# Gated product of two column halves, one core: the first row's load as two transfers of 32 and 96 partitions

## The chip, the cores and the metric

The kernel runs on one core of a Trainium2 chip. The metric is device time in microseconds (us) of one execution; three executions of the kernel before gave 932.57, 932.62 and 932.98, with a median of 932.62 us. One execution was recorded by the hardware profiler; its numbers are called the profile, and answers drawn from the recording are called the trace.

## The reference

```
x = randn(8192, 8192), float32
a, b = split(x, 2, axis=-1)          # columns 0..4095 and 4096..8191
out = a * (1 / (1 + exp(-b)))        # 8192 x 4096, float32
```

Every element of x is read once (268 MB) and every element of the output is written once (134 MB). There is no reuse: the sigmoid and the product take one element of each half.

## The kernel before, in words

**Tiles.** A tile is 256 rows of x: 128 partitions with two rows (`r`) each, so 64 KB of input and 32 KB of output per partition, 8 MB in and 4 MB out per tile. There are 32 tiles. Two input slots `xs[0]`, `xs[1]` and two output slots `os[0]`, `os[1]` are used in turn (`SLOTS = 2`). Neighbouring partitions of a tile lie 128 KB apart in x.

**One tile's work.** `load(i)` (L59 to L64) issues the input transfer on SP's queue. `work(i, ...)` (L72 to L93) has ACT put the sigmoid over the second column half in place (L82), and then DVE and POOL multiply the two halves into the output slot (L91); POOL takes 3/16 of the columns from tile 2 to tile 30, DVE the rest. `store(i, ...)` (L66 to L70) issues the output transfer on ACT's queue.

**Pieces.** Lists say how each tile is cut. `loads[0]` is `rows`: the first tile's input goes as two transfers, row 0 of every partition (32 KB each on 128 partitions, 4 MB) and then row 1. All other tiles load in one transfer of 8 MB. The first and the last tile are worked on in four pieces (`fourths`), and stored in two and three transfers.

**Order.** The loop issues `load(0)` and `load(1)`, and then for each tile its work, `load(i + 2)`, and its stores. `place` (L48 to L57) keeps the program order and drops all dependencies but the ones that it is given: a load waits for the multiplications that last read its slot (`free`, L62), the sigmoid waits for the transfers that bring its piece (`landed`, L78) and for the store that frees the output slot (`gone`, L79), a multiplication waits for the sigmoid, and a store for the multiplications.

**The early launch.** `_launch_early` (L110 to L120) takes the first transfer that SP issues, and it alone, out of the body and puts it ahead of the barrier at which the engines meet on entry, so that it is issued at the very start of the span. All other loads follow behind the barrier. `_close_on_sync` shortens the end and is not touched by the change.

**Transfers in the profile.** Each transfer of 128 partitions shows in the count of DMA packets as 144 packets: one data packet for each partition and 16 small ones of completion (33 loads make the 4752 packets of the input queue, 35 stores the 5040 of the output queue).

Of the kernel before, what the change touches and what calls it, by code (L numbers as in the profile page):

```python
# [8 lines left out]
def _tiles(ctx, tc, x, out):  # L9
    nc = tc.nc  # L10
    P = nc.NUM_PARTITIONS
    DEP = mybir.DependencyInfo(mybir.DependencyClass.Sync, mybir.DependencyReason.DATA)
    fp32 = mybir.dt.float32
    SIG = mybir.ActivationFunctionType.Sigmoid

    n_rows, n_cols = x.shape
    half = n_cols // 2
    R = 2
    SLOTS = 2
    n_tiles = n_rows // (P * R)  # L20
    x_g = x.rearrange("(g p h r) m -> g h p (r m)", p=P, h=2, r=R)
    out_g = out.rearrange("(g p h r) m -> g h p (r m)", p=P, h=2, r=R)

    pool = ctx.enter_context(tc.tile_pool(name="io", bufs=1))
    xs = [pool.tile([P, R * n_cols], fp32, name=f"x_sb{k}") for k in range(SLOTS)]
    os = [pool.tile([P, R * half], fp32, name=f"o_sb{k}") for k in range(SLOTS)]

    whole = [(0, 8)]
    rows = [(0, 4), (4, 8)]
    cut = half // 16 * 3  # L30
    at_once = [(0, 8, 0, half)]
    fourths = [(k, k + 2, k % 4 * half // 4, (k % 4 + 2) * half // 4) for k in range(0, 8, 2)]
    loads = [whole] * n_tiles
    works = [at_once] * n_tiles
    stores = [whole] * n_tiles
    behind = [0] * n_tiles
    loads[0] = stores[0] = rows
    works[0] = works[-1] = fourths
    stores[-1] = [(0, 4), (4, 6), (6, 8)]
    behind[-1] = 1  # L40

    def meet(a, b):
        return a[0] < b[1] and b[0] < a[1]

    traced = [[] for _ in range(SLOTS)]
    load_of, mul_of, store_of = {}, {}, {}

    def place(i, ins, *needs):  # L48


        kept = {n.ins.name for n in needs}
        for e in traced[i % SLOTS]:
            if e.ins.name not in kept:
                tc.declare_no_dep(ins.ins, e.ins, reason="follows from the waits that are kept")
        traced[i % SLOTS].append(ins)
        tc.keep_in_program_order(ins)
        return ins  # L57

    def load(i):  # L59
        for lo, hi in loads[i]:  # L60
            c = slice(lo * n_cols // 4, hi * n_cols // 4)
            free = [m for w, m in mul_of.get(i - SLOTS, []) if meet(w, (lo, hi))]  # L62
            ins = nc.sync.dma_start(out=xs[i % SLOTS][:, c], in_=x_g[i // 2, i % 2, :, c])  # L63
            load_of.setdefault(i, []).append(((lo, hi), place(i, ins, *free)))  # L64

    def store(i, lo, hi):  # L66
        c = slice(lo * half // 4, hi * half // 4)
        ins = nc.scalar.dma_start(out=out_g[i // 2, i % 2, :, c], in_=os[i % SLOTS][:, c])  # L68
        done = [m for w, m in mul_of[i] if meet(w, (lo, hi))]
        store_of.setdefault(i, []).append(((lo, hi), place(i, ins, *done)))  # L70

    def work(i, lo, hi, near, far):  # L72

        rows = xs[i % SLOTS].rearrange("p (r h m) -> p r h m", r=R, h=2)
        packed = os[i % SLOTS].rearrange("p (r m) -> p r m", r=R)
        r, c = slice(lo // 4, (hi + 3) // 4), slice(near, far)
        b = rows[:, r, 1, c]
        landed = [s for w, s in load_of[i] if meet(w, (lo, hi))]  # L78
        gone = [s for w, s in store_of.get(i - SLOTS, []) if meet(w, (lo, hi))]  # L79
        by_sigmoid = 0 < i < n_tiles - 1  # L80
        needs = [*landed, *(gone if by_sigmoid else ())]
        sig = place(i, nc.scalar.activation(out=b, in_=b, func=SIG), *needs)  # L82
        shares = [(nc.vector, near, far)]
        if by_sigmoid and i > 1:
            shares = [(nc.gpsimd, near, cut), (nc.vector, cut, far)]
        if by_sigmoid:
            for s in gone:
                tc.add_manual_dep(sig.ins, s.ins.name, DEP, reason="frees the output slot")
        for engine, a, z in shares:
            part = slice(a, z)  # L90
            mul = engine.tensor_mul(out=packed[:, r, part], in0=rows[:, r, 0, part], in1=rows[:, r, 1, part])  # L91
            place(i, mul, sig, *(() if by_sigmoid else gone))
            mul_of.setdefault(i, []).append(((lo, hi), mul))  # L93

    for i in range(SLOTS):
        load(i)
    for i in range(n_tiles):
        due = list(stores[i])
        for k, piece in enumerate(works[i]):
            work(i, *piece)  # L100
            ready = works[i][k - behind[i]][1] if k >= behind[i] else 0
            while len(stores[i]) > 1 and k < len(works[i]) - 1 and due[0][1] <= ready:
                store(i, *due.pop(0))
        if i + SLOTS < n_tiles:
            load(i + SLOTS)
        for lo, hi in due:
            store(i, lo, hi)
# [115 lines left out]
```

## Time and profile before

| what | value |
|---|---|
| median of three executions | 932.62 us |
| the profiled execution's own time | 932.69 us |
| its span, first to last instruction | 931.3 us |
| DVE, ACT, POOL busy | 232.3, 227.0, 299.5 us (25%, 24%, 32%) |
| moved by DMA | 402.67 MB, mean 432 GB/s over the span |
| first row of tile 0: ACT starts on it | 11.95 us |
| second row of tile 0: ACT starts on it | 21.67 us |
| tile 1: ACT starts on it | 46.39 us |
| last load issued, landed | 871.48, 911.8 us |

The profiled execution took 1.4 us more than its span, which is what lies around the first and the last instruction. In views by stretches, the DMA share is the time of the packets that start in the stretch, over 16 engines; short stretches can be over 1 or under it only because packets begin on one side of the border and end on the other. In the view of DMA issues, "us to landing" runs from the issue to the last completion.

### The profile page before, as it was taken

What the parts mean: (1) busy time and instruction counts of PE and PEld (TensorE: products, weight loads), DVE (VectorE), ACT (ScalarE), POOL (GpSimd) and SP (SyncE); (2) the same over time, 40 slices, a digit from 0 to 9 for tenths busy, and PEclk for the clock granted to TensorE, in tenths of its full rate; (3) what the DMA queues carried; (4) which work ended last, traced back from release to release, by engine and by line L of the source; (5) the groups of instructions that cost most, each with busy time, mean ns of one, the idle gap of its engine ahead of it and who ended that gap; (6) DMA issues with size and microseconds to landing.
All of it is one profiled execution on the core that took longest, in us unless ns stands there. A gap on an engine that the chain in (4) does not pass through costs nothing.

```text
span 931.3 us, 294 instructions
## 1 busy us (share of the span) xinstructions
DVE 232.3 (25%) x38; ACT 227.0 (24%) x39; POOL 299.5 (32%) x33
## 2 busy tenths in 40 slices
DVE  1133311333113331133321333203332033320233
ACT  2023332033320333202332023320233302333023
POOL 0004412444124441244422444224442244421440
DMA  9999999999999999999999999999999999999998
GB/s 405 450 405 450 428 450 408 470 405 428 450 428 450 405 462 417 428 450 426 452 405 436 442 428 450 418 457 408 428 450 426 452 407 466 411 428 450 425 453 383
DMA packets 9793, 402.67 MB, mean 432 GB/s; under 512 B 1088, under 2 KB 1088, under 8 KB 1088
## 3 DMA queue, kind: packets, MB, share of 16 engines
q1 hardware_dynamic: 4752, 268.44, 66.6%
q10 hardware_dynamic: 5040, 134.22, 33.4%
q14 instruction: 1, 0.01, 0.0%
HBM read 268.44 MB, written 134.22 MB: 432 GB/s over the span
## 4 chain that ended last, share of the span: by engine, by line
DMA 70%; POOL 16%; ACT 12%; DVE 2%; issue 0%; ACTq 0%; SPq 0%
DMA out_dram<-o_sb 61%; POOL o_sb L91 16%; ACT x_sb L82 12%; DMA x_sb<-in_x_dram 9%; DVE o_sb L91 2%; ACTq L68 0%; SPq L63 0%
## 5 line engine op out<-in xcount | busy, mean ns | idle before, releaser
L91 POOL TENSOR_TENSOR o_sb<-x_sb 128x1536 f32<-128x1536 f32 x29 | 299.3, 10321 | 600.7 <-ACT x_sb L82 600.7
L91 DVE TENSOR_TENSOR o_sb<-x_sb 128x6656 f32<-128x6656 f32 (+2 forms) x38 | 232.3, 6123 | 690.6 <-ACT x_sb L82 690.6
L82 ACT ACTIVATE x_sb<-x_sb 128x8192 f32<-128x8192 f32 (+1 forms) x38 | 225.7, 5950 | 692.9 <-DMA out_dram<-o_sb 632.8
L82 ACT ACT_TABLE_LOAD x1 | 1.3, 1283 | 0.8 <-PEq L207 0.8
L207 POOL MEMSET const-float32-0.0<- 128x1 f32 x1 | 0.1, 98 | 0.2 <-issue 0.2
L207 POOL MEMSET const-bfloat16-1.0<- 128x1 bf16 x1 | 0.1, 101 | 0.0
L207 POOL MEMSET const-uint8-127<- 128x1 uint8 x1 | 0.1, 101 | 0.0
L207 POOL MEMSET const-float32-1.0<- 128x1 f32 x1 | 0.1, 98 | 0.0
## 6 DMA issues: line engine op xcount, KB each, us to landing
out_dram<-o_sb ACTq DMA_DIRECT2D x30, 4096.0 KB, 40.5
x_sb<-in_x_dram SPq DMA_DIRECT2D x2, 4096.0 KB, 16.4
out_dram<-o_sb ACTq DMA_DIRECT2D x3, 2048.0 KB, 28.1
out_dram<-o_sb ACTq DMA_DIRECT2D x2, 1024.0 KB, 8.3
x_sb<-in_x_dram SPq DMA_DIRECT2D x31, 40.3
```

Of the source, the lines that this page charges most:

```text
L82: sig = place(i, nc.scalar.activation(out=b, in_=b, func=SIG), *needs)
L91: mul = engine.tensor_mul(out=packed[:, r, part], in0=rows[:, r, 0, part], in1=rows[:, r, 1, part])
L207: nc = _bacc.Bacc("TRN2", target_bir_lowering=False, num_devices=1)
```

## The change

The first transfer of the first tile, row 0 of its 128 partitions, is issued as two transfers: one of partitions 0 to 31 (1 MB) and one of partitions 32 to 127 (3 MB). All other transfers stay as they were. `_launch_early` still takes the first transfer that SP issues, which is now the one of 32 partitions; the one of 96 partitions is issued behind the barrier, ahead of row 1's. Both are entered in `load_of[0]`, so the sigmoids on row 0 wait for both.

```diff
         for lo, hi in loads[i]:
             c = slice(lo * n_cols // 4, hi * n_cols // 4)
             free = [m for w, m in mul_of.get(i - SLOTS, []) if meet(w, (lo, hi))]
-            ins = nc.sync.dma_start(out=xs[i % SLOTS][:, c], in_=x_g[i // 2, i % 2, :, c])
-            load_of.setdefault(i, []).append(((lo, hi), place(i, ins, *free)))
+            for p, q in [(0, 32), (32, P)] if i == 0 and lo == 0 else [(0, P)]:
+                ins = nc.sync.dma_start(out=xs[i % SLOTS][p:q, c], in_=x_g[i // 2, i % 2, p:q, c])
+                load_of.setdefault(i, []).append(((lo, hi), place(i, ins, *free)))
```

In the compiled order of instructions SP has one transfer more. The wait for the second transfer of row 0 is put on ACT's table load, the instruction ahead of the first sigmoid, which had no wait before; the sigmoid itself waits for the first. The transfers take the completion semaphores in turn, so from there on each transfer uses the next one in the circle.

## Prediction

> **What bounds the kernel now.** I read the page's row of DMA slices first, then the trace by stretches, then the first stretches' packets, and last the timeline of the start and the waits.
>
> The page's span, its DMA slices and its packet count:
>
> ```profile
> span 931.3 us, 294 instructions
> DMA  9999999999999999999999999999999999999998
> DMA packets 9793, 402.67 MB, mean 432 GB/s; under 512 B 1088, under 2 KB 1088, under 8 KB 1088
> ```
>
> No slice but the last has the 16 DMA engines under 90% busy, while no compute engine is busy for more than a third of the span. By stretches (columns: stretch, length, busy time and instructions of DVE, ACT and POOL, clock, DMA share, GB/s):
>
> ```profile
> 0.00:1.00 1.00, 0.00 (x0) 0.22 (x1) 0.20 (x4) 1.00 0.00 0
> 1.00:2.00 1.00, 0.00 (x0) 1.00 (x1) 0.00 (x0) 1.00 1.76 524
> ...
> 46.00:104.00 58.00, 15.78 (x2) 18.26 (x3) 10.32 (x1) 1.00 0.99 426
> 104.00:162.00 58.00, 14.19 (x2) 14.06 (x3) 20.64 (x2) 1.00 1.00 434
> 162.00:510.00 348.00, 85.11 (x12) 84.04 (x13) 123.86 (x12) 1.00 1.00 434
> 510.00:858.00 348.00, 85.11 (x12) 84.43 (x13) 123.86 (x12) 1.00 1.00 434
> ```
>
> The DMA engines move nothing in the first microsecond, and from then on their share is 1.00: 434 GB/s in every long stretch. There is no slack in them to take up a late start, so time that all of them lose anywhere is time on the end. The chain of waits names ACT and POOL between the stores, but the DMA engines work on other tiles' transfers meanwhile.
>
> How one engine works is read from the packets that start between 1 and 2 us and between 2 and 11.2 us:
>
> ```profile
> DMA packets 16, 0.52 MB, mean 524 GB/s; under 512 B 0, under 2 KB 0, under 8 KB 0
> q1 hardware_dynamic: 16, 0.52, 175.7%
> ```
>
> ```profile
> DMA packets 112, 3.67 MB, mean 399 GB/s; under 512 B 0, under 2 KB 0, under 8 KB 0
> q1 hardware_dynamic: 112, 3.67, 92.3%
> ```
>
> The first 16 packets, one per engine, took 1.76 us each (175.7% of 1 us). The other 112 packets of row 0 took 0.923 x 9.2 us x 16 / 112 = 1.21 us each. A packet is 32 KB, one partition's row, so an engine writes one partition at a time, at 27 GB/s, and sixteen do it side by side. The timeline of the start:
>
> ```profile
> 0.78 1.28 ACT L82 ACT_TABLE_LOAD   x1 [0.78 <-PEq L207]
> 11.95 3.71 ACT L82 ACTIVATE x_sb<-x_sb 128x2048 f32<-128x2048 f32 x2 [9.89 <-DMA x_sb<-in_x_dram]
> 18.42 0.37 ACTq L68 DMA_DIRECT2D out_dram<-o_sb  x1
> 21.67 3.71 ACT L82 ACTIVATE x_sb<-x_sb 128x2048 f32<-128x2048 f32 x2 [6.00 <-DMA x_sb<-in_x_dram]
> 28.13 89.45 SPq L63 DMA_DIRECT2D x_sb<-in_x_dram  x4
> 46.39 7.03 ACT L82 ACTIVATE x_sb<-x_sb 128x8192 f32<-128x8192 f32 x1 [21.01 <-DMA x_sb<-in_x_dram]
> ```
>
> Row 1 is there 21.67 - 11.95 = 9.72 us after row 0: 4.19 MB at 432 GB/s, with 128 partitions open to the 16 engines.
>
> **The change part by part.** The sum is made on the profiled execution: span 931.3 us, plus 1.4 us around it, is its 932.69 us, 0.07 us over the median of 932.62 us. I add the differences to the median.
>
> *One more issue on SP.* An issue takes 0.33 us and they follow 0.38 us apart (0.78, 1.16). The 96-partition transfer takes the place at 0.78; row 1's moves to about 1.16 and tile 1's to about 1.54. The engines have row 0 until 11.3 us, so this costs nothing; without that cover it would cost 0.38 us.
>
> *The gap between the two parts.* The early launch now carries 1 MB, not 4. At full rate that is two packets an engine, done by 1.0 + 1.76 + 1.21 = 4.0 us. The 96-partition transfer is issued at 0.78, and by the first one's lag (1.0 to 2.0 us from issue to the first packets) its packets are ready by 2.8 us. Covered by 1.2 us; bare, it would cost up to 0.8 us, the delay of the issue.
>
> *More packets.* 144 packets become 48 and 112, so 9809 in all, 16 more completions. All 68 transfers have their completions inside the 434 GB/s; one more is under 0.1 us.
>
> *A quicker first packet?* A transfer with a third of the packets (48, not 144) could start sooner. The most there is to gain: the idle 1.0 us, and 1.76 - 1.21 = 0.55 us of the first round, 1.55 us together; the least is nothing. The issue on SP takes 0.37 us for this transfer and 0.36 to 0.37 us for stores whose row is 16 or 32 KB, which all have 128 partitions, so no row shows that fewer partitions are quicker. I take 0.
>
> *The table load's wait.* ACT's table load, 1.28 us, ran at 0.78 under the load. It now waits until the second part has landed, and the sigmoids of row 0 wait behind it: their start slips by 1.28 us on top of any delay of the load, and the first store with them, from 18.42 to 19.7 us. Who waits: DVE, then ACT's queue. Row 1's work starts on its own landing (21.67 us), and the load of tile 2 at 28.13 us waits for row 1's product. The engines hold loads until tile 1 lands at 46.4 us, so the first store changes places with load packets and costs nothing. If this cover went, it would cost 1.28 us.
>
> *The semaphores' turn.* Each steady load waits for the semaphore of the load four tiles before, as it did, under another number. It is long done: nothing.
>
> *The rate of the two parts.* This carries the sum. In all 68 transfers of the trace the partitions reached are all 128; no row shows what sixteen engines do when all write into the same 32. From one side: a packet keeps its 1.21 us, as an engine writes one partition at a time and 32 are still twice sixteen. Then 0. From the other: the rate goes with the partitions reached, and each part takes as long as a whole row, 9.72 us. The 32 then cost 9.72 - 2.43 = 7.29 us more, the 96 cost 9.72 - 7.29 = 2.43 us more, together +9.72 us. The low end has the one-packet rate for it. Against it: that rate was seen only with the sixteen writing over the whole memory, eight partitions to an engine (8 packets each in a row), and sixteen streams pushed into a quarter of it most likely share what leads there. Single partitions take 27 GB/s, so the high end, 108 GB/s into 32 of them, is too harsh as well. Neither row is nearer, and I take the middle, half the lanes: the 32 at half rate cost 2.43 us more, and of the 96 the upper 64 have the other half of the lanes, 9.72 us in place of 7.29, again +2.43 us. Sum +4.86 us. It is not won back: an engine that falls behind has the same share of each later transfer as the others.
>
> [...]
>
> Median 932.62 + 4.86 = 937.5 us.
>
> **The rivals.**
>
> *Rate unchanged* (the other side: not slower). The place is the first 4 us; the packets of the 32 partitions keep 1.21 us. For it: the constant 1.21 us for one partition. Against it: the crowding above. It decides from a mean packet under about 1.44 us, since (1.44 - 1.21) x 8 packets an engine in row 0 is 1.84 us. Time 932.6 us, down to 931.1 us if all of the 1.55 us of the start is won; even that is less than 0.2% (1.87 us, about what a measurement of this kernel can tell from no change).
>
> *Uneven engines.* If the 96 partitions are dealt in blocks of six, some engines share a lane through all their packets and others do not; the slowest one sets every landing and the end. Such an engine would run the whole row at half rate: +9.72 us, 942.3 us. For it: all engines have an equal share, so there is no balancing. Against: those that finish early leave the lanes to the late ones.
>
> *The start runs dry.* If row 0 is so late that row 1's product and the load of tile 2 come after tile 1 has landed, the engines idle. The margin is 46.4 - 28.1 = 18 us, more than the 9.72 + 1.28 us that the worst above adds. Beyond it, over 943 us.
>
> *The change does not do what it says*, one transfer being launched early as before: excluded by the order of instructions, where SP has 32 partitions ahead of the barrier and 96 behind.
>
> **How the numbers follow.** Shared lanes, the forecast, loss 2.4 to 7 us (935 to 939.6): 0.50. Uneven engines, loss 7 to 9.7 us (939.6 to 942.4): 0.23. Rate unchanged or loss under 1.87 us: 0.21, of it 0.02 faster by more than 0.2% through something not seen in these rows. Beyond 942.4 us: 0.06. The range runs from 932.3 to 942.4 us; it leaves out the 0.06 and some 0.06 of quicker starts. Slower 0.79, same 0.19, faster 0.02. The likeliest case's own range is 935.0 to 939.6 us.
>
> **What would show it.** Right: packets that start in the first 6 us take 1.8 to 2.5 us each, the first sigmoid starts at about 11.95 + 4.86 + 1.28 = 18.1 us right behind a table load of 1.28 us, row 1's at 26.5 us and tile 1's at 51 us; from there all stretches at 434 GB/s, only later. Wrong: row 1 at 21.7 us, with 1.21 us packets; then the change is harmless. It would also be wrong if the delay of the start is there and a later stretch runs over 434 GB/s to win it back, or if a later stretch falls under 1.00 DMA share.

## The result and the profile after

The changed kernel takes 968.93 us (median of six executions, 965.92 to 974.65) against 932.67 us before (932.57 to 933.25): a ratio of 1.0391, with a 95% interval of 1.0372 to 1.0410. The forecast was 937.5 us, with a range up to 942.4 us. The profiled execution took 966.64 us with a span of 965.2 us.

The page of the changed kernel, its span, DMA slices and packets:

```profile
span 965.2 us, 297 instructions
DMA  9999999999999999999999999999999999999997
DMA packets 9809, 402.67 MB, mean 417 GB/s; under 512 B 1104, under 2 KB 1104, under 8 KB 1104
```

The same bytes in the 16 packets more that were forecast, the DMA engines again busy throughout, and 417 GB/s in place of 432. The timeline of the start (start, length, engine and operation; in brackets the idle time before and what ended it):

```profile
21.73 1.28 ACT L83 ACT_TABLE_LOAD   x1 [21.73 <-DMA x_sb<-in_x_dram]
23.03 3.71 ACT L83 ACTIVATE x_sb<-x_sb 128x2048 f32<-128x2048 f32 x2
29.50 0.38 ACTq L69 DMA_DIRECT2D out_dram<-o_sb  x1
31.37 3.71 ACT L83 ACTIVATE x_sb<-x_sb 128x2048 f32<-128x2048 f32 x2 [4.63 <-DMA x_sb<-in_x_dram]
37.84 0.36 ACTq L69 DMA_DIRECT2D out_dram<-o_sb  x1
55.49 7.03 ACT L83 ACTIVATE x_sb<-x_sb 128x8192 f32<-128x8192 f32 x1 [20.42 <-DMA x_sb<-in_x_dram]
```

The work on row 1 starts 9.70 us later than before (31.37 against 21.67), tile 1 9.10 us later (55.49 against 46.39), and row 0 waits for its landing and then for a table load of 1.28 us. The packets that start between 2 and 18 us show why row 0 is late:

```profile
DMA packets 121, 3.44 MB, mean 215 GB/s; under 512 B 16, under 2 KB 16, under 8 KB 16
q1 hardware_dynamic: 121, 3.44, 99.5%
```

In such a row stand the queue (q1 carries SP's loads, q10 ACT's stores), its packets, MB, and the time of its packets as a share of 16 engines over the stretch. 16 of the 121 are the completions of the first part. The other 105 packets of 32 KB took 0.995 x 16 us x 16 / 105 = 2.43 us each on average, where they took 1.21 us before: half rate, in the first part and in the second. That is the 9.7 us. But the span is 33.9 us longer. The rest is in the stretches behind (columns as in the prediction):

```profile
46.00:104.00 58.00, 15.79 (x2) 14.06 (x2) 10.32 (x1) 1.00 1.00 431
104.00:162.00 58.00, 14.18 (x2) 14.06 (x2) 20.64 (x2) 1.00 1.00 420
162.00:510.00 348.00, 83.00 (x12) 84.35 (x12) 118.49 (x12) 1.00 1.00 424
510.00:858.00 348.00, 80.12 (x12) 79.20 (x12) 118.93 (x12) 1.00 1.00 423
```

The DMA share is 1.00 as before, yet from 104 us on the engines move 420 to 424 GB/s in place of 434, long after the split transfer is done. The chain of waits shows it as a store that takes longer (start, length):

```profile
128.39 42.02 DMA out_dram<-o_sb
170.41 0.02 issue
170.44 7.04 ACT x_sb L83
177.47 0.07 issue
177.54 10.33 POOL o_sb L92
187.90 42.47 DMA out_dram<-o_sb
```

Two tiles take 187.90 - 128.39 = 59.5 us; before, they took 58.0 us (a store from 117.26, the next from 175.26). The pages say which packets are slow: loads take 67.3% of 965.2 us in place of 66.6% of 931.3, about 29 us more on each engine, of which row 0's half rate is some 9; stores take 32.3% in place of 33.4%, under 2 us more. The last load is issued at 904.60 us in place of 871.48: of its 33.1 us of delay, 9.1 were there at tile 1, and 24.0 came in the 28 tiles between, 0.86 us a tile.

So there are two questions: why row 0 runs at half rate, and why a disturbed start makes 28 later tiles slower. The second is worth more, and nothing in the prediction had a price for it.

### The profile page after: what moved, and what is told of

The parts are those of the page before. It is cut to its first block, busy times and chain, and to the rows that moved or that the text cites. A ratio compares the mean times of both kernels' runs of the same rounds, so it can differ in the third digit from the quotient of the medians.

```text
span 965.2 us, 297 instructions
## 1 busy us (share of the span) xinstructions
DVE 232.3 (24%) x38; ACT 227.0 (24%) x39; POOL 299.6 (31%) x33
## 3 DMA queue, kind: packets, MB, share of 16 engines
q1 hardware_dynamic: 4768, 268.44, 67.3%
q10 hardware_dynamic: 5040, 134.22, 32.3%
## 4 chain that ended last, share of the span: by engine, by line
DMA 68%; POOL 15%; ACT 12%; DVE 2%; another core or an unknown queue 2%; issue 0%; ACTq 0%; SPq 0%
DMA out_dram<-o_sb 61%; POOL o_sb L92 15%; ACT x_sb L83 12%; DMA x_sb<-in_x_dram 7%; DVE o_sb L92 2%; ACTq L69 0%; SPq L64 0%; ACTq L83 0%
```

## The experiments

The theories, in the order in which they came up. **A**: the half rate of row 0 leaves the sixteen engines out of step with one another, and that lasts. **B**: row 0's work, and with it the first store, is late. **C**: the side effects of having two transfers. **D**: addresses in memory. **E**: a later start of the loads. **F** and **M**: the moment of the first store against the engines' packets. **G**: a table load that runs beside the transfers. **P**: a first store that comes one load packet later, so that the loads run a packet ahead of the stores. Of the longer edits the code shows the lines that matter.

### Split by columns; work late; halves; a small hold-up

*columns*, both parts on 128 partitions:

```diff
+            q = (c.stop - c.start) // 8 * 5
+            for d in [slice(c.start, c.start + q), slice(c.start + q, c.stop)] if i == 0 and lo == 0 else [c]:
```

> Row 0's load is again two transfers, but cut by columns (20 KB and 12 KB of each row) so that both reach all 128 partitions. The extra issue, the turned semaphores and the wait on ACT's table load stay. Theory A (the partitions reached: half rate in row 0, and by it the sixteen DMA engines out of step for the rest): 932.6 us within 2 us, row 1 at about 21.7 us. Theory B (the delay of row 0's work, which puts the stores behind the loads for the whole run): the delay left is 1.28 us, so at most a few us, under 937 us. Theory C (the side effects of having two transfers): like the changed kernel, 960 us or more.

Four executions took 938.8, 938.8, 958.0 and 960.6 us. The full rate was back, row 1 at 21.84 us, so the half rate hangs on the partitions. But even the two quicker executions are 6 us above the kernel before, and the other two over 25 us: something besides the half rate makes the run slow, and not alike in every execution.

*late*, row 0's sigmoid also waits for row 1:

```diff
+            tc.add_manual_dep(sig.ins, load_of[0][1][1].ins.name, DEP, reason="row 0 waits for row 1")
```

> The kernel before, unsplit, but the work on row 0 waits until row 1 has landed too: the table load starts at about 21.7 us and the first store is issued at about 29.4 us, as late as in the changed kernel (29.50 us), while the loads run undisturbed. Theory A: the DMA engines are never short of work, 932.6 us within 2 us. Theory B: the steady stretches fall to about 424 GB/s, 950 us or more.

936.87 us (ratio 1.0051, 1.0036 to 1.0066), the first store issued at 29.54 us, steady stretches at 434 GB/s. Lateness alone (B) does not make the long loss. Between 98 and 103 us this kernel moved only 315 GB/s: no load packet starts from 95 to 101.5 us, so the load queue ran empty there once, which matters below.

*halves*, `[(0, 64), (64, P)]` in place of `[(0, 32), (32, P)]`:

> The same change with 64 and 64 partitions in place of 32 and 96. If the rate goes with the partitions' lanes and 64 reach no more of them than 32, row 0 runs at half rate throughout, as in the changed kernel: row 1 at about 31.4 us. Theory A: then the engines' order decides: 942 us if all are held up alike, 955 to 975 us if they fall out of step as with 32 and 96. Theory B: 960 us or more, since row 0's work is as late. If the rate goes with the count of partitions and not with the lanes, both parts also run at half rate, and this does not tell the two apart.

963.75, 968.67, 971.66 and 982.61 us in four executions, row 1 at 32.34 us. 64 partitions are no quicker than 32: 113 packets of 32 KB that start between 2 and 20 us took 2.5 us each (0.994 x 18 us x 16 / 113; 16 completions are left out).

*skew*, one small transfer more behind row 0:

```diff
+            if i == 0 and lo == 0:
+                nc.sync.dma_start(out=os[1][0:4, 0:4096], in_=x_g[0, 0, 0:4, 0:4096])
```

> The kernel before, unsplit, with one small transfer more behind row 0: 4 partitions of 16 KB into a slot that is not in use yet. It should go to only a few of the sixteen DMA engines and hold those up by 0.6 to 2.4 us; all else starts on time. Theory A (engines out of step make the steady stretches slower): clearly more than the direct 2.4 us, 940 to 970 us, with steady stretches under 430 GB/s. Theory B: 933 to 935 us, steady stretches at 434 GB/s.

934.44 us (ratio 1.0022, 1.0013 to 1.0032), steady stretches at 434 GB/s. Holding up a few engines cost the hold-up and no more here. A, as it was put, is in doubt from here on: three engines are held up to the end (13 load packets of tile 4 start from 99.4 to 100.3 us and the other three of the first sixteen after 102.8 us, and at tile 30 it is the same), and it costs nothing further.

### The same delay in step; starting again in step; other addresses

*uniform*, a whole extra row ahead of row 0, and *resync*, the changed kernel whose third tile's load waits for the second to land:

```diff
+            if i == 0 and lo == 0:
+                nc.sync.dma_start(out=os[1], in_=x_g[0, 0, :, c])
```

```diff
+                if i == 2:
+                    tc.add_manual_dep(ins.ins, load_of[1][0][1].ins.name, DEP, reason="starts in step")
```

> The kernel before, unsplit, with a whole extra row (4 MB over 128 partitions, into the second output slot before its first use) loaded ahead of row 0. It adds the same 9.7 us to the start as the half rate does in the changed kernel, and makes row 0's work as late, but all sixteen engines stay in step. Theory A (out of step after row 0): 932.6 + 9.7 = 942 to 946 us, steady stretches at 434 GB/s. Theory E (a start that is 9.7 us later is enough, since the first stores then meet the loads at another point): 960 us or more, steady stretches under 428 GB/s.

942.46 us (942.44 to 942.50): 9.85 us more than before, and nothing behind it. E falls.

> The changed kernel, 32 and 96 partitions, but the load of tile 2 also waits until tile 1 has landed, so that the load queue runs empty once and all engines start tile 2 together. Row 0 keeps its half rate: row 1 at about 31.4 us. Theory A: the steady loss goes away; 932.6 + 9.7 + about 3 us for the empty queue = 944 to 950 us, steady stretches at 434 GB/s. If the loss has another carrier than the engines' order at that point (the addresses in memory, the semaphores), it stays: 965 us or more.

944.23 us (943.56 to 944.70), steady stretches at 434 GB/s with row 0 still at half rate (row 1 at 31.16 us). The 25 us behind row 0 are not caused by the split as such: here one emptying of the load queue, with no load packet starting from 55 to 58.6 us, was enough to keep them away. *late* had such an emptying by chance.

*contig_split* and *contig_whole*, tiles of 256 neighbouring rows (`"(g h p r) m -> g h p (r m)"` for x and the output), with and without the split:

> The changed kernel with another assignment of rows to tiles: a tile is 256 neighbouring rows, so that neighbouring partitions lie 64 KB apart in x and not 128 KB (32 KB and not 64 KB in the output); sizes, order and the split are the same. Theory A alone says nothing of addresses: 960 us or more again. Theory D (engines out of step are slow only because loads and stores then meet at bad addresses in memory): the loss changes by much, about 942 to 946 us if it goes.

> The kernel before with the same other assignment of rows to tiles and no split, to tell what the assignment alone does. Both theories: 932.6 us within 2 us, since the engines are in step and never idle; a different figure would say that the addresses count in step too.

972.26 us and 932.68 us: as with the other assignment. With the distance between neighbouring partitions halved nothing changes, so D has nothing for it.

### The table load, and the size of the lanes

*split_table* and *columns_table* are the changed kernel and *columns* with a sigmoid of one column at the very start, so that the table load no longer waits:

```diff
+    warm = pool.tile([P, 1], fp32, name="warm")
+    tc.keep_in_program_order(nc.vector.memset(warm, 0.0))
+    tc.keep_in_program_order(nc.scalar.activation(out=warm, in_=warm, func=SIG))
```

> The changed kernel, 32 and 96 partitions, with a sigmoid of one column at the very start, so that the table load is done early and no longer waits for the second part; row 0's work starts 1.28 us sooner, at its half-rate landing. Theory A (the half rate of row 0 alone puts the engines out of step): 960 us or more still. Theory F (the step is lost because the first stores come at another moment against the loads, for which 1.28 us is enough): could fall to 942 to 948 us.

> The cut by columns, which ran at 938 to 961 us, with the same early table load. What is left against the kernel before is one more transfer and a first row that lands about 0.2 us later. Theory F: 932.6 to 935 us in all runs. If having two transfers is itself the trigger, the scatter of 938 to 961 us stays.

941.80 us (941.68 to 941.94) and 932.69 us (ratio 1.0001, 0.9991 to 1.0010). This divides the result: with the table load early, 32 and 96 partitions cost 941.80 - 932.63 = 9.2 us, and the other 968.93 - 941.80 = 27.1 us hang on the table load's place, which puts back row 0's work by 1.28 us. The scatter of *columns* goes too (932.57 to 932.96 us in ten executions), and the extra transfer, packets and semaphores cost nothing.

*delay1*, the kernel before with 1.3 us more of ACT's time ahead of row 0's work:

```diff
+        if i == 0 and lo == 0:
+            lead = nc.scalar.activation(out=os[1][:, :1300], in_=xs[0][:, :1300], func=SIG)
+            tc.keep_in_program_order(lead)
```

> The kernel before, unsplit and at full rate, with one more sigmoid of 1300 columns into an unused slot ahead of row 0's work, about 1.28 us, so that only the work on row 0 and its store come later by what the table load's wait costs. Theory A: 932.6 us within 1 us. Theory F: slower and scattered, 934 to 960 us.

932.66 us (ratio 1.0000, 0.9990 to 1.0010). F fell by this run, or so it seemed: 1.3 us of delay did nothing here. (0.5 us more does, as *delay2* shows below.)

*sixteen*, `[(0, 16), (16, P)]`:

> 16 and 112 partitions in place of 32 and 96, to size the rate by the partitions reached. If 16 neighbouring partitions reach half the lanes of 32: the first packet of each engine takes about 4.8 us (four engines to a lane) where the 32 took 2.4 us, the 112 go on at half rate, 7 packets of 2.42 us, and row 1 is there at about 21.7 + 3.6 + 8.5 = 33.8 us. If the half rate has nothing to do with the lanes reached (a fixed penalty of a part), the first packets take about 2.4 us and row 1 is there at about 31.4 us. The total should be 942 us or more in any case, and about 965 to 975 us if the engines fall out of step.

972.29 us (two executions). The first packets took 3.78 us each, against 2.24 us for 32 partitions, 2.33 us for 64 (*halves*, 2.183 us x 16 / 15) and 1.76 us for 128, so those of the 16 are the slowest; but row 1 was there at 31.56 us and not at 33.8, so the 112 made good what the 16 lost. My count of four engines to a lane is not borne out in size.

### The moment of the first store

One view made the runs comparable. A store of row 0 gives each engine one first packet of 16 KB, so counting the packets of ACT's queue (q10) in a short stretch counts engines. In the changed kernel, 32.5 to 34 us and then 34.4 to 36 us:

```profile
q1 hardware_dynamic: 16, 1.05, 161.5%
q10 hardware_dynamic: 4, 0.07, 10.3%
```

```profile
q1 hardware_dynamic: 10, 0.66, 94.5%
q10 hardware_dynamic: 12, 0.20, 28.7%
```

Four engines take the store's first packet at about 33.0 us; the other twelve take one more load packet of 64 KB (2.42 us) and come to the store at about 35.2 us. In *split_table*, 32.5 to 34 us:

```profile
q1 hardware_dynamic: 16, 1.05, 161.2%
q10 hardware_dynamic: 16, 0.26, 41.1%
```

All sixteen take it together. The store of the changed kernel was issued at 29.50 us and has its first packet 3.5 us later, just as the engines end a load packet. In no run here does a first store have a packet sooner than 3.4 us after its issue; by that, the store of *split_table*, issued at 28.35 us, was ready before any engine ended its packet. Three kernels move only this moment. *delay2* is *delay1* with 1900 columns; *split_later* is the changed kernel with the same `lead` of 1150 columns; *table_delay* is *split_table* with a `lead` of 1300 columns.

> The kernel before, unsplit, full rate, no wait on the table load; the extra sigmoid ahead of row 0's work has 1900 columns in place of 1300, so that the first store is issued at about 20.25 us and not at 19.77 us. Theory M (the moment: a store's packets can start about 3.5 us after its issue, and if that moment falls among the engines' packet ends, some take the store's packet first and others one more load packet, and from there they are a packet out of step): ready at about 23.7 us, in the middle of the engines' packet ends at 23.6 to 24.0 us, so the first store's packets start in two groups 2.4 us apart, and the time is 934 to 970 us with scatter. Theory G (a table load that runs beside the transfers does it): 932.6 us within 1 us.

> The changed kernel, 32 and 96 partitions, with the table load's wait as it is, and an extra sigmoid of 1150 columns ahead of row 0's work, about 1.2 us: the first store is issued at about 30.7 us and can start at about 34.2 us, between the engines' packet ends (32.6 to 33.2 and 35.0 to 35.6 us). Theory M: all sixteen start it together at about 35.2 us, steady stretches at 434 GB/s, 942 to 944 us, some 25 us faster than the changed kernel though more work is done. Theory G: 960 us or more.

> The changed kernel with the early table load (941.8 us) and an extra sigmoid of 1300 columns ahead of row 0's work, which puts the first store back to about 29.7 us, where the changed kernel has it. Theory M: ready at about 33.15 us, among the engines' packet ends at 33.0 to 33.3 us: out of step again, 955 to 975 us with scatter. Theory G: 942 us.

*delay2* took 967.27 us (ratio 1.0348, 1.0306 to 1.0390), *table_delay* 971.17 us (1.0429, 1.0366 to 1.0492), *split_later* 961.28 us (1.0305, 1.0290 to 1.0320). G falls in both kernels whose table load is early: *table_delay* is slow again, and the kernel before, whole, loses 35 us to a sigmoid of 1.8 us, where one of 1.3 us cost nothing. *delay2* issues its first store 0.40 us after *delay1*, and its second within 0.1 us of it. In *delay2* the first store packets, 23 to 24.5 us and then 25.5 to 27 us:

```profile
q10 hardware_dynamic: 2, 0.03, 5.1%
```

```profile
q10 hardware_dynamic: 14, 0.23, 35.6%
```

But M falls as well, in *split_later*: there all sixteen started the store together, as the count from 34.8 to 36 us shows, and the loss came all the same:

```profile
q10 hardware_dynamic: 16, 0.26, 51.0%
```

What the slow runs share is not that the engines start the store apart, but that engines come to the first store one load packet later. *delay3* (2900 columns) does that to all sixteen in the kernel before. *few* asks what slows the packets then; it puts the sigmoid on 64 columns of a row only, from tile 2 to tile 30, and leaves the rest of b as it is; each multiplication still waits for its sigmoid.

```diff
+        few = b[:, :, 0:64] if by_sigmoid and i > 1 else b
+        sig = place(i, nc.scalar.activation(out=few, in_=few, func=SIG), *needs)
```

> The kernel before, unsplit, full rate, early table load; the extra sigmoid ahead of row 0's work has 2900 columns, so that the first store is issued at about 21.0 us and can start at about 24.5 us, between the engines' packet ends: all sixteen take one more load packet first and start the store together at about 26.2 us. Theory M (engines apart from one another): in step, 932.6 us within 1 us. Theory P (the first store one load packet later, so that the loads turn to the next tile ahead of the stores, is enough even with all engines together): 945 to 970 us with scatter.

> The changed kernel, but from tile 2 to tile 30 the sigmoid is put over 64 of each row's 4096 columns only (the rest is multiplied as it is): ACT works 0.3 us a tile in place of 7.03 us, and the transfers keep sizes and order. If the slow load packets at the turn of a tile come from ACT's accesses beside the loads, they go and the steady stretches run at 434 GB/s, 942 to 946 us. If they come from the transfers alone, the stretches stay under 428 GB/s and the time over 955 us.

*delay3* took 953.04 us (ratio 1.0215, 1.0195 to 1.0236). Its first store packets, 25.5 to 27 us, and its stretches:

```profile
q10 hardware_dynamic: 16, 0.26, 40.7%
```

```profile
104.00:162.00 58.00, 14.19 (x2) 12.85 (x3) 20.64 (x2) 1.00 1.01 433
162.00:220.00 58.00, 14.18 (x2) 13.59 (x2) 20.64 (x2) 1.00 1.01 432
220.00:278.00 58.00, 14.19 (x2) 14.06 (x2) 20.64 (x2) 1.00 1.00 425
510.00:858.00 348.00, 83.66 (x12) 84.35 (x12) 119.13 (x12) 1.00 1.00 423
```

P's forecast comes true and M's does not: whole transfers, full rate, the engines together at the first store, and the loss follows. Row 1's work, the second store and the load of tile 2 stand within 0.1 us of where the kernel before has them, so only row 0's work and its store come later, and that is enough for the loss. How it makes the loss is not shown, and it takes time: from 46 to 220 us *delay3* moves 431 to 433 GB/s, and 425 only after that. The engines come apart over the same tiles: the first sixteen load packets of tile 4 start from 98.8 to 99.7 us, those of tile 9 from 245.0 to 247.6 us. The first slow packets come while they are still together: the next sixteen of tile 4, all started from 101.4 to 102.4 us, took 2.65 us each. So in the slow stretches the engines are apart here too, but being apart isn't enough, as *skew* shows.

*few* took 967.67 us (two executions), at 423 GB/s: ACT's accesses are not the cause of the slow packets. Those of DVE and POOL were not varied.

The runs side by side (engines that took the first store early, after one 64 KB load packet of tile 1, and late, after two; GB/s from 162 to 510 us):

| kernel | first store issued, us | early / late | median, us | GB/s |
|---|---|---|---|---|
| before | 18.42 | 16 / 0 | 932.6 | 434 |
| delay1 | 19.77 | 16 / 0 | 932.7 | 434 |
| delay2 | 20.17 | 2 / 14 | 967.3 | 420 |
| delay3 | 20.98 | 0 / 16 | 953.0 | 426 |
| uniform | 28.24 | 16 / 0 | 942.5 | 434 |
| split_table | 28.35 | 16 / 0 | 941.8 | 434 |
| table_delay | 29.43 | 11 / 5 | 971.2 | 420 |
| changed kernel | 29.50 | 4 / 12 | 968.9 | 424 |
| split_later | 30.61 | 0 / 16 | 961.3 | 424 |

The time does not grow with the number of late engines; five are as bad as sixteen. *halves* (13 early), *few* (6), *contig_split* (3) and *sixteen* (2), all slow, have late engines as well. So have *resync* (8 early) and *late* (none early), which moved 434 GB/s once their load queue had run empty. One run doesn't fit a plain rule: the one late engine of the profiled run of *columns* (15 of its first store packets came from 23.4 to 24.3 us) went with a steady 434 GB/s in that execution, while two other executions of it took 20 us more.

Where the time is lost within a tile can be seen at one turn. In the changed kernel, the packets that start from 113 to 116 us, at the turn from one tile's load to the next:

```profile
q1 hardware_dynamic: 16, 1.05, 102.0%
q10 hardware_dynamic: 4, 0.13, 10.1%
```

The 16 load packets of 64 KB took 1.02 x 3 us = 3.06 us each. In the kernel before, a stretch of 3 us with one load packet of each engine (134.5 to 137.5 us):

```profile
q1 hardware_dynamic: 16, 1.05, 80.6%
```

There they took 2.42 us. Why load packets become slow at the turn when the first store came late is open: it isn't ACT's work (*few*), the distance between partitions in memory (*contig_split*) or the engines being apart as such (*skew*). A slow packet counts as busy for all of its 3.06 us, so the DMA share stayed at 1.00.

## Why the prediction was wrong

**What bounds the kernel**: right, though 434 GB/s holds from 104 us on only: the stretch from 46 to 104 us has 426 in the lines shown there. The DMA engines are busy throughout, and *uniform* gives back 9.7 us of added transfer as 9.85 us of time.

**One more issue, the gap, the packets, the semaphores**, each at nothing: right, shown by *columns_table* at a ratio of 1.0001. In the changed kernel itself there is no gap between the two parts, as the share of 99.5% from 2 to 18 us shows.

**A quicker first packet**, taken at 0: right. No packet of the changed kernel starts before 1 us either, and the first ones took 2.24 us in place of 1.76.

**The rate of the two parts**, +4.86 us: that both parts lose was right, the size was not. Measured in *split_table*, it is 9.2 us, close to the high end of 9.72 that I called too harsh. The 32 partitions ran at about half rate, as put: their two packets an engine took 2.24 and 2.54 us in place of 1.76 and 1.21, 1.8 us more where I had 2.43. The term that was mis-sized is the second: the 96 were to lose 2.43 us, on my assumption that the upper 64 have lanes of their own; their six packets an engine took 2.41 us each on average, about 7 us more. No run shows lanes, or which partitions would share one: the 4.86 us was my choice between 0 and 9.72. In its place the runs show about half rate for 32, 64 and 96 partitions alike (2.4, 2.5 and 2.41 us a packet against 1.21); why is open.

**The table load's wait**, at nothing: this is the step that made the forecast wrong, by 27.1 us. I wrote that the first store "changes places with load packets and costs nothing", and priced the cover's loss at 1.28 us. The cover was there: the engines had loads until tile 1 landed. But to change places with a load packet is the very thing that costs: when only the first store's moment moved (*delay1*, *delay2*, *delay3*), the time went from 932.7 us to 967.3 and 953.0 us, and *table_delay* brought the loss back with the table load early. The loss did not come where the load queue ran empty once (*resync*, 434 GB/s from 104 us on); by what means it lasts elsewhere is not shown. In the counts above an engine comes to the store only at the end of a 2.42 us load packet: in the changed kernel four engines at 33.0 to 33.2 us, the other twelve at 35.0 to 35.5 us. I had not asked at which packet's end that would be.

**The rivals.** *Rate unchanged* is out: 2.43 us a packet. *Uneven engines* had nearly the right price for row 0 (942.3 us) by the wrong way: all sixteen engines were slowed alike, and their packets start within 1.2 us of one another through row 0. *The start runs dry* did not happen: the load of tile 2 was issued with the second store, at 37.84 us, 17.65 us before tile 1 was there. None of them had the slow stretches in it; the 0.06 left for more than 942.4 us stood for engines that run dry, which they did not.

**What would show it.** I meant to find a wrong forecast by a stretch whose DMA share falls under 1.00. The share stayed at 1.00 while the GB/s fell from 434 to 424; the column to watch was the last one.

## What to carry to other kernels

In a kernel that keeps its DMA engines full, a delay of an early store that is hidden by other work can still cost: here 1.15 us (28.35 to 29.50 us) cost 27, and the loss stayed away where the load queue ran empty once (*resync*, 944.23 us). Judge such a change by the packets of the first store and by GB/s in the long stretches, not by the DMA share. Load with all 128 partitions: 32, 64 or 96 of them went at about half the rate here (2.4, 2.5 and 2.41 us for 32 KB, against 1.21), and a cut by columns cost nothing with the table load early. And when an instruction gets a second wait, look where that wait is put: here it fell on a table load that had been free, and moving the table load ahead took back 27 of the 36 us.

## What the hardware did that I had not expected

- Partitions 32 to 127 loaded at half rate (2.41 us for 32 KB, against 1.21), though they are 96 of the 128; 16 partitions started at 3.78 us a packet.
- Under a full load queue a store's first packet started 3.5 us after its issue (29.50 to 33.0 us), while the first load of the kernel needed 1.0 us.
- After a first store that came one load packet late, load packets at the turn of a tile became slow (3.06 us in place of 2.42 in the changed kernel at 113 us), and the rate fell (424 GB/s in place of 434), in *delay3* only after 220 us.
- Engines that are apart were not slow for that: in *skew* three of sixteen ran behind the others to the end, at a steady 434 GB/s.
- With a sigmoid of 1.3, 1.8 or 2.6 us ahead of the first store the kernel before took 932.7, 967.3 or 953.0 us.
